# A hybrid attention block on one core: matmul operands moved to multiples of 256 bytes

## The chip, the cores and the metric

The kernel runs on one core of a Trainium2 chip. The metric is the device time of one execution in microseconds (us). A profile of one execution gives the times of single instructions. The engines are TensorE (PE in the rows, its weight loads PEld), VectorE (DVE), ScalarE (ACT), GpSimd (POOL) and SyncE (SP, which here only issues DMAs).

## The reference

One encoder layer over 512 tokens of width 1024 in float32, with 16 learned meta tokens placed ahead of them (528 rows in all):

```
h = rmsnorm(concat(meta, x));  proj = h @ w_in      # 1024 x 5120: q,k,v of two branches, two gates
A: neighbourhood attention, 8 heads of 64: each query sees 16 columns x 8 rows of the grid
   (8 x 64 tokens) with a learned bias, and the 16 meta tokens
B: differential attention, 4 heads: softmax(q1 k1) - lam * softmax(q2 k2) over all 528 keys,
   rotary positions, a norm per head
x = x + (sigmoid(g_na) * (A @ w_na) + sigmoid(g_df) * (B @ w_df)) @ w_o
x = x + (silu(h2 @ w_gate) * (h2 @ w_up)) @ w_down   # h2 = rmsnorm(x), inner width 2816
return rmsnorm(x) without the meta tokens
```

## The kernel before

Everything is held transposed: a tile has 128 features on the partitions and the tokens along the row. The host lays the tokens out column block by column block, 256 tokens, then the 16 meta tokens, then the other 256.

Every float32 factor of a dense product is split into a rounded high part and the remainder, both float32r, and one product is three matmuls (`mm3`, lines 137, 139, 141): high x high, high weight x low activation, low weight x high activation. Every matmul instruction loads its own 128x128 weights. Weights come in pieces of 8 blocks by DMA (`wraw`), and ACT and DVE split them (`whi`, `wlo`).

Names of the matmul groups, with the moving operand behind the arrow; all with 512 columns where nothing else is said:

- `pk<-xh` and `pv<-xh`: keys and values (`dense_full`), 528 tokens as two runs of 264 columns (`HALF`), 192 pairs each.
- `pq<-xh` (192) and `pg<-xh` (384): queries and gates (`dense_real`, `gate_block`). They need the 512 real tokens alone, so `rcols` reads two runs of 256 out of the row of 528, and results are handled as two runs (`v2`).
- `s<-kd`: scores. Branch B (line 506) takes two runs of 264 into two PSUM banks, 64 pairs; branch A (line 609) one run of 272, 64 matmuls.
- `tp`, `mp`: transposes of the softmax rows `w`. `pvd<-ath` (48) and `pvn<-ath` (64 of 256 columns): probabilities x values.
- `pd<-odh` (96), `pn<-onh` (96), `po<-mh` (192): output projections.
- `pf<-xgh`: gate and up of the feed-forward, 22 x 2 x 8 x 3 = 1056 matmuls. `pdn<-gh`: down, 462; `pdh<-gh`: its last block of outputs, 132 matmuls of 256 columns.

`xh` and `xl` are [128, 8, 528] float32r, so feature block k starts k x 2112 bytes into the tile.

The program has two phases. In the first (`run`), eight units (four heads of B, four pairs of heads of A, in turn) go through scores, softmax, transposes and value products in slots; between those PE does dense work of the next unit from a generator (`fill`). In the second (`phase_b`) the dense layers follow one another. The tile framework orders each engine's instructions, hands out addresses (pools stack up from the left end of a partition's row of SBUF or down from its right end) and makes a new tile in a tag wait until an old tile of that tag is free.

At the start `setup` loads x into eight tiles `xr` in the tags `ath` and `atl`, makes `xh`, `xl` and the sums of squares, and loads `lv` (the lambda vectors) into a tile of its own. `stats` makes the norm's factor `R` (from `ssq` by way of `ms`, `dg`, `rp`), folds it into the rotary tables `cos` and `sin`, finishes the first unit's keys and queries (`later`: rope by way of `sw`, then copies `kd` and `qs` by DMA), and multiplies the lambda vectors (`lt`, line 305). `build_bm` (POOL, line 593) adds bias (`toep`) and mask into `bm` for each head of branch A.

Of the kernel before, what the change touches and what calls it, by code (L numbers as in the profile page):

```python
# [18 lines left out]
P = 128  # L19
# [5 lines left out]
HALF = LT // 2  # L25
GRID_W = 64
# [9 lines left out]
KCOL = [0, 128, 272, 400]  # L36
MCOL = 256
# [13 lines left out]
V_PACK = [[(0, 64, 384), (64, 256, 0), (256, 264, 512)],  # L51
          [(0, 8, 520), (8, 200, 192), (200, 264, 448)]]
# [11 lines left out]
class Kernel:  # L64
# [133 lines left out]
    def setup(self):  # L198
        nc, a = self.nc, self.a
        cp, at = self.cp, self.attn  # L200
        self.unit_blocks = []
        for h in range(4):
            self.unit_blocks += [(16 + h, 12 + h, 20 + h), (4 + h, h, 8 + h)]
        self.wplan()

        vec = cp.tile([P, 25], F32, name="vec")
        nc.gpsimd.dma_start(vec, a["vec"])
        self.g1, self.g2, self.g3 = vec[:, 0:8], vec[:, 8:16], vec[:, 16:24]
        A1 = self.A1
# [23 lines left out]
        self.cos = at.tile([P, LT], F32, name="cos")  # L233
        self.sin = at.tile([P, LT], F32, name="sin")
# [10 lines left out]
        ssq = at.tile([P, LT], F32, name="ssq", tag="w", bufs=2)  # L245
        nc.scalar.activation(ssq, xr[0], AF.Square)
        for k in range(1, KT):
            sq = at.tile([P, LT], F32, name="sq", tag="e", bufs=3)
# [24 lines left out]
        self.R = A1.tile([P, LT], F32, name="R")  # L273
        self.na = 0
        self.nv = 0


    def stats(self, later):
# [8 lines left out]
        dg = self.attn.tile([P, LT], F32, name="dg", tag="e", bufs=3)  # L287
# [12 lines left out]
        lt = self.sm.tile([P, 2, 64], F32, name="lt")  # L300
# [12 lines left out]
    def dense_full(self, name, outs):  # L313
# [23 lines left out]
    def gate_block(self, dst, between=None):  # L337
# [7 lines left out]
        self.nc.vector.tensor_tensor(out=v2(dst), in0=v2(o[0]), in1=rcols(self.R), op=ALU.mult)  # L345
# [21 lines left out]
    def v_dense(self, st, diff):  # L367
# [11 lines left out]
    def v_transpose(self, st, diff):  # L379
# [3 lines left out]
        for c in range(NCH):  # L383
            k0 = KCOL[c] if diff else c * P
# [13 lines left out]
        k0 = MCOL if diff else T  # L398
        nc.tensor.transpose(mp[0:NMETA, :P], vt[:, k0:k0 + NMETA], self.ident)
# [26 lines left out]
    def k_dense(self, u, st, diff, defer=None):  # L426
# [24 lines left out]
    def q_dense(self, u, st, diff, defer=None):  # L451
# [40 lines left out]
    def d_scores(self, h, st, s):  # L492
# [11 lines left out]
        for i in range(2):  # L504
# [5 lines left out]
        e = at.tile([P, LT], F32, name="e", tag="e", bufs=3)  # L510
        nc.scalar.activation(e.rearrange("p (i n) -> p i n", i=2), sc[:, :, :HALF], AF.Exp, bias=m,  # L511
                             accum_out=l[:, c:c + 1])
        st["e"].append(e)
        if c == 1:
# [6 lines left out]
            w = at.tile([P, LT], F32, name="w", tag="w", bufs=2)  # L521
# [18 lines left out]
    def d_pv(self, h, st, am):  # L540
# [9 lines left out]
        sq = self.attn.tile([P, LT], F32, name="sqh", tag="e", bufs=3)  # L550
# [4 lines left out]
    def d_norm1(self, h, st, o, sq):  # L555
# [5 lines left out]
        dg = self.attn.tile([P, LT], F32, name="dg", tag="e", bufs=3)  # L561
# [11 lines left out]
    def build_bm(self, head):  # L573
# [4 lines left out]
        for b in range(4):  # L578
# [6 lines left out]
            nc.gpsimd.memset(bm[:, b, MCOL - lo:MCOL - lo + NMETA], 0.0)  # L585
# [12 lines left out]
    def n_scores(self, u, st, s):  # L598
# [11 lines left out]
        e = at.tile([P, LT], F32, name="en", tag="e", bufs=3)  # L610
# [7 lines left out]
        w = at.tile([P, LT], F32, name="w", tag="w", bufs=2)  # L618
# [23 lines left out]
    def n_pv(self, u, st, hd, am, ath, atl):  # L642
# [16 lines left out]
        tmp = self.attn.tile([P, LT], F32, name="otmp", tag="e", bufs=3)  # L659
# [72 lines left out]
    def run(self):  # L732
# [14 lines left out]
        self.attn = sat.enter_context(tc.tile_pool(name="attn", bufs=1))  # L747
        self.sstg = ExitStack()
# [49 lines left out]
    def phase_b(self, sA2):  # L798
        tc, nc, a = self.tc, self.nc, self.a
        with ExitStack() as top:  # L800
# [8 lines left out]
            for m in range(KT):  # L809
                nc.gpsimd.dma_start(v2(x1[:, m]), rcols(a["x"][m]))  # L810
# [170 lines left out]
def v2(t):  # L981
    return t.rearrange("p (b n) -> p b n", b=2)


def rcols(t):

    return bass.AP(t.tensor, t.offset, [list(t.ap[0]), [272, 2], [1, 256]])


# [14 lines left out]
def _layout(x, meta_tokens, mix_norm, w_in, na_rpb, lambda_q1, lambda_k1, lambda_q2, lambda_k2,  # L1004
# [4 lines left out]
    xc = np.concatenate([xp[:256], f(meta_tokens), xp[256:]], axis=0)  # L1009
# [6 lines left out]
    pos = np.concatenate([NMETA + perm[:256], np.arange(NMETA), NMETA + perm[256:]]).astype(np.float32)  # L1016
# [51 lines left out]
```

## Time and profile before

| | |
|---|---|
| median of 3 runs | 793.13 us (792.68 to 793.28) |
| the profiled execution | 792.06 us, its span 790.3 us |
| instructions in the span | 10578, of them 4002 matmuls |
| PE busy | 774.2 us (98%) |
| DVE, ACT, POOL busy | 460.2, 310.5, 65.4 us |
| mean DMA rate | 113 GB/s |

Matmuls are pipelined: a matmul of 512 columns takes some 390 ns from start to end in the trace, while the next one starts some 230 ns after it. The step from one start to the next is therefore what to read, not the duration.

### The profile page before, as it was taken

Reading aid. Unit: us, or ns where it says so; the run is one execution under the profiler, and the core shown is the slowest. Engines: PE = TensorE matmul, PEld = TensorE weight load, DVE = VectorE, ACT = ScalarE, POOL = GpSimd, SP = SyncE. Lnnn points to the kernel's source line nnn. Section 1 sums busy time; section 2 is a strip of 40 time slices with the busy share of each in tenths; the row PEclk is TensorE's granted clock in tenths of the full one; section 3 lists DMA queues with packets and bytes.
Section 4 is the critical chain, followed back from the end, with each engine's and each line's share of the span. In section 5 each row is a group of like instructions: output and inputs, shape, how many; then the busy total and the mean of one; then the engine's idle time right before and its main releaser. Section 6 shows DMA issues by size and latency. Waiting matters only on the chain.

```text
span 790.3 us, 10578 instructions
## 1 busy us (share of the span) xinstructions
PE 774.2 (98%) x4002; PEld 651.8 (82%) x4002; DVE 460.2 (58%) x892; ACT 310.5 (39%) x522; POOL 65.4 (8%) x140
## 2 busy tenths in 40 slices
PE   7999999999999999999999999999999999999995
PEld 5899889989898888878887888888888888888885
DVE  6868898798788766657443644444444545322314
ACT  6345554554555547323432432323232324322311
POOL 5300110110011000020220000000000000000100
PEclk9999999999999999999999999999999999999998
DMA  7474644434463412262232222332323234332313
GB/s 266 141 199 106 163 114 129 126 112 119 119 173 95 122 55 79 86 206 91 97 106 80 91 96 86 103 102 84 99 88 107 80 100 148 105 99 88 103 45 106
DMA packets 29922, 89.20 MB, mean 113 GB/s; under 512 B 4208, under 2 KB 6272, under 8 KB 29872
## 3 DMA queue, kind: packets, MB, share of 16 engines
q1 hardware_dynamic: 27904, 84.41, 35.3%
q0 software_dynamic: 1136, 3.34, 1.4%
q10 hardware_dynamic: 832, 0.79, 0.3%
q8 instruction: 31, 0.51, 0.3%
q14 instruction: 19, 0.16, 0.1%
HBM read 71.45 MB, written 2.10 MB: 93 GB/s over the span
## 4 chain that ended last, share of the span: by engine, by line
PE 95%; DVE 2%; DMA 1%; ACT 1%; issue 1%; SPq 0%; DVEq 0%; ACTq 0%
PE pf L137 10%; PE pf L141 10%; PE pf L139 10%; PE pdn L137 4%; PE pdn L139 4%; PE pdn L141 4%; PE pg L137 4%; PE pg L141 4%; PE pg L139 4%; PE s L506 2%; PE pq L141 2%; PE pv L137 2%; PE pv L139 2%; PE pv L141 2%; PE po L141 2%; PE po L137 2%
## 5 line engine op out<-in xcount | busy, mean ns | idle before, releaser
L114 ACT CAST whi<-wraw 128x1024 fp32r<-128x1024 f32 (+2 forms) x123 | 126.8, 1031 | 305.0 <-issue 112.7
L115 DVE TENSOR_TENSOR wlo<-wraw,whi 128x1024 fp32r<-128x1024 f32 (+2 forms) x123 | 147.5, 1199 | 89.4 <-ACT whi L114 84.7
L137 PE MATMUL pf<-xgh,whi 128*128 128x512 f32 x352 | 140.0, 398 | 0.0
L141 PE MATMUL pf<-xgh,wlo 128*128 128x512 f32 x352 | 139.2, 395 | 0.0
L139 PE MATMUL pf<-xgl,whi 128*128 128x512 f32 x352 | 139.2, 395 | 0.0
L139 PEld LDWEIGHTS pf<-xgl,whi 128*128 128x128 f32 x352 | 66.1, 188 | 16.1 <-issue 0.2
L141 PEld LDWEIGHTS pf<-xgh,wlo 128*128 128x128 f32 x352 | 66.1, 188 | 16.0
L137 PEld LDWEIGHTS pf<-xgh,whi 128*128 128x128 f32 x352 | 66.1, 188 | 15.9 <-issue 0.2
L139 PE MATMUL pdn<-gl,whi 128*128 128x512 f32 x154 | 59.9, 389 | 0.0
L137 PE MATMUL pdn<-gh,whi 128*128 128x512 f32 x154 | 59.9, 389 | 0.0
L141 PE MATMUL pdn<-gh,wlo 128*128 128x512 f32 x154 | 59.9, 389 | 0.0
L966 DVE TENSOR_TENSOR u<-pf,R 128x512 f32<-128x512 f32 x22 | 15.2, 691 | 68.8 <-PE pf L141 68.8
L137 PE MATMUL pg<-xh,whi 128*128 128x512 f32 x128 | 52.8, 412 | 0.4 <-DVE vt L374 0.4
L978 POOL TENSOR_TENSOR ssq<-ssq,sq 128x512 f32<-128x512 f32 x11 | 19.4, 1763 | 381.9 <-ACT sq L977 381.9
L139 PE MATMUL pg<-xl,whi 128*128 128x512 f32 x128 | 50.9, 397 | 0.0
L141 PE MATMUL pg<-xh,wlo 128*128 128x512 f32 x128 | 50.6, 395 | 0.0
L964 DVE TENSOR_TENSOR s<-pf,R 128x512 f32<-128x512 f32 x22 | 15.2, 690 | 45.1 <-PE pf L141 45.1
L147 ACT CAST ath<-tp 128x256 fp32r<-128x256 f32 (+1 forms) x48 | 20.5, 443 | 42.7 <-PE tp L631 22.0
L141 PEld LDWEIGHTS pdn<-gh,wlo 128*128 128x128 f32 x154 | 28.9, 188 | 6.1
L137 PEld LDWEIGHTS pdn<-gh,whi 128*128 128x128 f32 x154 | 28.9, 188 | 6.0
L139 PEld LDWEIGHTS pdn<-gl,whi 128*128 128x128 f32 x154 | 28.9, 188 | 5.9
L511 ACT ACTIVATE e<-s,m 128x528 f32<-128x528 f32 x32 | 22.5, 703 | 23.8 <-DVE m L509 23.4
(221 smaller groups left out, 1506.2 us busy)
## 6 DMA issues: line engine op xcount, KB each, us to landing
wraw<-in_w_in_dram SPq DMA_DIRECT2D x39, 512.0 KB, 3.5
wraw<-in_w_gate_dram SPq DMA_DIRECT2D x22, 512.0 KB, 3.2
wraw<-in_w_up_dram SPq DMA_DIRECT2D x22, 512.0 KB, 3.2
kd<-khl SPq DMA_DIRECT2D x32, 264.0 KB, 4.1
wraw<-in_w_down_dram SPq DMA_DIRECT2D x16, 512.0 KB, 3.5
qs<-qhl SPq DMA_DIRECT2D x32, 128.0 KB, 2.8
wraw<-in_w_o_dram SPq DMA_DIRECT2D x8, 512.0 KB, 3.3
wraw<-in_w_down_dram SPq DMA_DIRECT2D x8, 384.0 KB, 3.1
```

What stands on the lines that cost most here:

```text
L114: nc.scalar.copy(hi[:, k:k + h], raw[:, k:k + h])
L115: eng.tensor_tensor(out=lo[:, k:k + h], in0=raw[:, k:k + h], in1=hi[:, k:k + h].bitcast(F32), op=ALU.subtract)
L137: nc.tensor.matmul(outs[i], wh, rhs[i][0], start=start, stop=False)
L139: nc.tensor.matmul(outs[i], wh, rhs[i][1], start=False, stop=False)
L141: nc.tensor.matmul(outs[i], wl, rhs[i][0], start=False, stop=stop)
L147: self.nc.scalar.copy(hi, src)
L506: nc.tensor.matmul(sc[:, i, :HALF], qs[:, q], kd[:, p, i * HALF:(i + 1) * HALF], start=p == 0, stop=p == 1)
L511: nc.scalar.activation(e.rearrange("p (i n) -> p i n", i=2), sc[:, :, :HALF], AF.Exp, bias=m, accum_out=l[:, c:c + 1])
L964: nc.vector.tensor_tensor(out=s, in0=pgu[0], in1=R2, op=ALU.mult)
L966: nc.vector.tensor_tensor(out=u, in0=pgu[1], in1=R2, op=ALU.mult)
L978: (nc.gpsimd if m < n - 1 else nc.vector).tensor_tensor(out=ssq, in0=ssq, in1=sq, op=ALU.add)
```

## The change

Sizes and places in SBUF change; the arithmetic is the same but for the order of the keys. The meta tokens come last in the row, so the 512 real tokens are one run. Rows of 528 words that a matmul reads get a stride of 576 words (2304 bytes). Keys and values are computed in runs of 256 and 272 columns. The scores of branch B go into 528 neighbouring PSUM words that begin in the middle of one bank, so that run 0 ends that bank and run 1 begins the next, and DVE and ACT read them as one run. `cos`, `sin` and `R` share a tile in another pool; two of the eight `xr` tiles go to the tag `kd`; `lv` goes to the tag `toep` (one buffer) and `lt` to the tag `sw` (two buffers); a pad of 56 words is put at the right end of the row, under everything else there. Branch A keeps the meta keys in the middle of its key row (`NA_META`), with one more evacuation for it.

```diff
+LP = 576
+RUNS = [(0, 256), (256, 528)]
...
-        self.xh = A1.tile([P, KT, LT], F32R, name="xh")
-        self.xl = A1.tile([P, KT, LT], F32R, name="xl")
+        self.xh = A1.tile([P, KT, LP], F32R, name="xh")[:, :, :LT]
+        self.xl = A1.tile([P, KT, LP], F32R, name="xl")[:, :, :LT]
+        rows = A1.tile([P, 1600], F32, name="rows")[:, :3 * LT].rearrange("p (i n) -> p i n", i=3)
+        self.cos, self.sin, self.R = rows[:, 0], rows[:, 1], rows[:, 2]
...
-            xb = at.tile([P, 4, LT], F32, name="xr", tag=tag, bufs=1)
-            xr += [xb[:, i] for i in range(4)]
+            xb = at.tile([P, 3, LT], F32, name="xr", tag=tag, bufs=1)
+            xr += [xb[:, i] for i in range(3)]
+            xr.append(at.tile([P, LP], F32, name="xr", tag="kd", bufs=3)[:, :LT])
...
-        lv = self.sm.tile([P, 4, 64], F32, name="lv")
+        lv = at.tile([P, 4, 64], F32, name="lv", tag="toep", bufs=1)
...
-        lt = self.sm.tile([P, 2, 64], F32, name="lt")
+        lt = self.at_f32("lt", "sw", 2)[:, :P].rearrange("p (i n) -> p i n", i=2)
...
-        outs += [p[:, :HALF] for p in ps]
+        outs += [p[:, :b - a] for p, (a, b) in zip(ps, RUNS)]
         for k in range(KT):
             self.mm3(outs, wh[:, k], wl[:, k],
-                     [(self.xh[:, k, i * HALF:(i + 1) * HALF], self.xl[:, k, i * HALF:(i + 1) * HALF])
-                      for i in range(2)], k == 0, k == KT - 1)
+                     [(self.xh[:, k, a:b], self.xl[:, k, a:b]) for a, b in RUNS], k == 0, k == KT - 1)
...
-            self.mm3([o], wh[:, k], wl[:, k], [(rcols(self.xh[:, k]), rcols(self.xl[:, k]))],
+            self.mm3([ps], wh[:, k], wl[:, k], [(self.xh[:, k, :T], self.xl[:, k, :T])],
...
-            kd = self.attn.tile([P, 2, LT], F32R, name="kd", tag="kd", bufs=3)
+            kd = self.attn.tile([P, 2, LP], F32R, name="kd", tag="kd", bufs=3)[:, :, :LT]
...
-        for i in range(2):
+        sc = sc.rearrange("p i n -> p (i n)")[:, T - RUNS[0][1]:][:, :LT]
+        for r0, r1 in RUNS:
             for p in range(2):
-                nc.tensor.matmul(sc[:, i, :HALF], qs[:, q], kd[:, p, i * HALF:(i + 1) * HALF],
-                                 start=p == 0, stop=p == 1)
+                nc.tensor.matmul(sc[:, r0:r1], qs[:, q], kd[:, p, r0:r1], start=p == 0, stop=p == 1)
-        nc.vector.tensor_reduce(out=m, in_=sc[:, :, :HALF], op=ALU.max, axis=AX.XY, negate=True)
+        nc.vector.tensor_reduce(out=m, in_=sc, op=ALU.max, axis=AX.X, negate=True)
...
+        rp = es.enter_context(tc.tile_pool(name="rp", bufs=1, side="right"))
+        nc.gpsimd.memset(rp.tile([P, 56], F32, name="pad"), 0.0)
...
-                nc.gpsimd.dma_start(v2(x1[:, m]), rcols(a["x"][m]))
+                nc.gpsimd.dma_start(x1[:, m], a["x"][m][:, :T])
...
+    def at_f32(self, name, tag, bufs):
+        return self.attn.tile([P, LP], F32, name=name, tag=tag, bufs=bufs)[:, :LT]
```

The tiles in the tags `e`, `w` and `sw` are made by `at_f32` too. The value evacuation for branch A has 4 pieces in place of 6, the key evacuation 3 in place of 2.

## Rows read from the trace of the kernel before

**Rows 1.** The chain that ended last: shares of the span by engine.
```profile
PE 95%; DVE 2%; DMA 1%; ACT 1%; issue 1%; SPq 0%; DVEq 0%; ACTq 0%
```
**Rows 2.** What PE waited for, us in total, times, longest.
```profile
PE pq L141 <- DVE wlo L115: 1.4, 1, 1.4
```
**Rows 3.** Windows: busy us of PE, PEld, DVE, ACT, POOL; granted clock, DMA share, GB/s.
```profile
368.00:408.00 40.00, 40.00 (x179) 33.10 (x177) 19.70 (x23) 15.96 (x22) 10.73 (x6) 1.00 0.30 97
450.00:615.00 165.00, 165.00 (x708) 132.83 (x708) 74.46 (x89) 48.78 (x60) 0.00 (x0) 1.00 0.28 93
```
**Rows 4.** Timeline of PE, start and duration: `po` 64 matmuls, `pf` 62, first and last.
```profile
367.65 0.39 PE L141 MATMUL po<-mh,wlo 128*128 128x512 f32 x1
...
381.93 0.39 PE L141 MATMUL po<-mh,wlo 128*128 128x512 f32 x1
...
469.66 0.40 PE L141 MATMUL pf<-xgh,wlo 128*128 128x512 f32 x1
...
483.90 0.40 PE L137 MATMUL pf<-xgh,whi 128*128 128x512 f32 x1
```
**Rows 5.** Timeline of PE: 12 of `pvd`, 24 of `pg` (then `pvn`), 63 of `pd`.
```profile
84.41 0.39 PE L137 MATMUL pvd<-ath,vhl 128*128 128x512 f32 x1
...
86.98 0.39 PE L141 MATMUL pvd<-ath,vhl 128*128 128x512 f32 x1
...
308.65 0.39 PE L137 MATMUL pg<-xh,whi 128*128 128x512 f32 x1
...
314.21 0.39 PE L646 MATMUL pvn<-aM,VM 128*128 128x512 f32 x1
...
321.63 0.39 PE L137 MATMUL pd<-odh,whi 128*128 128x512 f32 x1
...
335.82 0.39 PE L141 MATMUL pd<-odh,wlo 128*128 128x512 f32 x1
```
**Rows 6.** Timeline of PE: 13 pairs of `pk`, 12 of `pv`, one of `s`, 25 `pdh`.
```profile
42.36 0.40 PE L141 MATMUL pk<-xh,wlo 128*128 128x264 f32 x2
...
45.29 0.41 PE L141 MATMUL pk<-xh,wlo 128*128 128x264 f32 x2
...
87.21 0.40 PE L137 MATMUL pv<-xh,whi 128*128 128x264 f32 x2
...
90.12 0.42 PE L609 MATMUL s<-kd,qs 128*128 128x272 f32 x2
90.37 0.38 PE L631 MATMUL tp<-ident,w 128*128 128x128 f32 x2
...
770.04 0.28 PE L141 MATMUL pdh<-gh,lo 128*128 128x256 f32 x1
...
772.84 0.28 PE L141 MATMUL pdh<-gh,lo 128*128 128x256 f32 x1
```
**Rows 7.** Timeline of the start, POOL and DVE.
```profile
11.59 5.50 POOL L593 TENSOR_TENSOR bm<-toep,mask 128x192 f32<-128x192 f32 x6 [4.67 <-DMA toep<-in_rpb_dram]
...
16.55 0.62 DVE L305 CUSTOM_DVE_ANT_0 lt<-lv 128x64 f32<-128x64 f32 x1
...
17.72 1.21 DVE L115 TENSOR_TENSOR wlo<-wraw,whi 128x1024 fp32r<-128x1024 f32 x1
...
19.48 0.21 DVE L305 CUSTOM_DVE_ANT_0 lt<-lv 128x64 f32<-128x64 f32 x1
...
19.77 5.69 POOL L593 TENSOR_TENSOR bm<-toep,mask 128x192 f32<-128x192 f32 x6 [1.82 <-DMA toep<-in_rpb_dram]
```
**Rows 8.** DMA issues: count, KB each, median us from issue to landing.
```profile
kd<-khl SPq DMA_DIRECT2D x32, 264.0 KB, 4.1
...
qs<-qhl SPq DMA_DIRECT2D x32, 128.0 KB, 2.8
```
**Rows 9.** Timeline of SP and PE at the first scores.
```profile
45.76 0.59 SPq L355 DMA_DIRECT2D qs<-qhl  x1
...
49.70 0.65 PE L506 MATMUL s<-kd,qs 128*128 128x264 f32 x4
```

More of the change, by code (lines that the diff above doesn't have):

```diff
@@ L34 @@
 LAM_INIT = 0.8 - 0.6 * math.exp(-0.3 * 0)
-KCOL = [0, 128, 272, 400]
-MCOL = 256
+KCOL = [0, 128, 256, 384]
+MCOL = T
+NA_META = 256
 NA_W = 272
@@ L49 @@
            [(80, 208, 0), (16, 80, 128), (208, 272, 192), (0, 16, 256)]]
-V_PACK = [[(0, 64, 384), (64, 256, 0), (256, 264, 512)],
-          [(0, 8, 520), (8, 200, 192), (200, 264, 448)]]
+V_PACK = [[(0, 64, 384), (64, 256, 0)], [(0, 192, 192), (192, 272, 448)]]
 GBLK = [(0, 1), (1, 2), (2, 3), (0, 3)]
@@ L232, in setup @@
         self.wemit = 2
-        self.cos = at.tile([P, LT], F32, name="cos")
-        self.sin = at.tile([P, LT], F32, name="sin")
         for k in range(KT):
@@ L243, in setup @@
         nc.sync.dma_start(self.sin, a["rope"][1])
-        ssq = at.tile([P, LT], F32, name="ssq", tag="w", bufs=2)
+        ssq = self.at_f32("ssq", "w", 2)
         nc.scalar.activation(ssq, xr[0], AF.Square)
         for k in range(1, KT):
-            sq = at.tile([P, LT], F32, name="sq", tag="e", bufs=3)
+            sq = self.at_f32("sq", "e", 3)
             nc.scalar.activation(sq, xr[k], AF.Square)
@@ L260, in setup @@
         make_identity(nc, self.ident)
-        lv = self.sm.tile([P, 4, 64], F32, name="lv")
+        lv = at.tile([P, 4, 64], F32, name="lv", tag="toep", bufs=1)
         nc.gpsimd.dma_start(lv, a["lam"].partition_broadcast(P))
-        self.mask = at.tile([P, 3, 4, 8], F32, name="mask")
+        self.mask = at.tile([P, 4, 4, 8], F32, name="mask")[:, 0:3]
         nc.gpsimd.dma_start(self.mask, a["mask"])
@@ L272, in setup @@
         self.lv = lv
-        self.R = A1.tile([P, LT], F32, name="R")
         self.na = 0
@@ L286, in stats @@
         yield 1.3
-        dg = self.attn.tile([P, LT], F32, name="dg", tag="e", bufs=3)
+        dg = self.at_f32("dg", "e", 3)
         self.diag(dg[:W].rearrange("p (c q) -> p c q", c=6), y, W, 6)
@@ L344, in gate_block @@
                 yield from between
-        self.nc.vector.tensor_tensor(out=v2(dst), in0=v2(o[0]), in1=rcols(self.R), op=ALU.mult)
+        self.nc.vector.tensor_tensor(out=dst, in0=o[0], in1=self.R[:, :T], op=ALU.mult)
         yield 0.65
@@ L371, in v_dense @@
         vt = self.stg.tile([P, LT], F32, name="vt", tag="vt", bufs=1)
-        for i in range(2):
-            for a, b, o in [(0, HALF, i * HALF)] if diff else V_PACK[i]:
+        for i, (lo, hi) in enumerate(RUNS):
+            for a, b, o in [(0, hi - lo, lo)] if diff else V_PACK[i]:
                 nc.vector.tensor_tensor(out=vt[:, o:o + b - a], in0=outs[i][:, a:b],
-                                        in1=self.R[:, i * HALF + a:i * HALF + b], op=ALU.mult)
+                                        in1=self.R[:, lo + a:lo + b], op=ALU.mult)
         st["vt"] = vt
@@ L383, in v_transpose @@
         for c in range(NCH):
-            k0 = KCOL[c] if diff else c * P
+            k0 = c * P
             nc.tensor.transpose(tp[:, c * P:(c + 1) * P], vt[:, k0:k0 + P], self.ident)
@@ L397, in v_transpose @@
         mp = self.tp.tile([P, T], F32, name="mpv", tag="tp")
-        k0 = MCOL if diff else T
-        nc.tensor.transpose(mp[0:NMETA, :P], vt[:, k0:k0 + NMETA], self.ident)
+        nc.tensor.transpose(mp[0:NMETA, :P], vt[:, T:T + NMETA], self.ident)
         if diff:
@@ L415, in rope @@
         nc = self.nc
-        sw = self.attn.tile([P, LT], F32, name="sw", tag="sw", bufs=2)
+        sw = self.at_f32("sw", "sw", 2)
         for i in range(4):
@@ L419, in rope @@
             nc.sync.dma_start(sw[32 * i:32 * i + 32, :n], raw[32 * j:32 * j + 32, :n])
-        shp = (lambda t: v2(t)) if n == T else (lambda t: t)
-        nc.vector.tensor_tensor(out=shp(raw[:, :n]), in0=shp(raw[:, :n]), in1=cos, op=ALU.mult)
-        nc.vector.tensor_tensor(out=shp(sw[:, :n]), in0=shp(sw[:, :n]), in1=sin, op=ALU.mult)
+        nc.vector.tensor_tensor(out=raw[:, :n], in0=raw[:, :n], in1=cos[:, :n], op=ALU.mult)
+        nc.vector.tensor_tensor(out=sw[:, :n], in0=sw[:, :n], in1=sin[:, :n], op=ALU.mult)
         nc.vector.tensor_tensor(out=raw[:, :n], in0=raw[:, :n], in1=sw[:, :n], op=ALU.add)
@@ L431, in k_dense @@
         raw = self.stg.tile([P, LT], F32, name="raw", tag="raw", bufs=2)
-        for i in range(2):
-            s = slice(i * HALF, (i + 1) * HALF)
+        for i, (a, b) in enumerate(RUNS):
             if diff:
-                nc.scalar.copy(raw[:, s], outs[i])
-            else:
-                nc.vector.tensor_tensor(out=raw[:, s], in0=outs[i], in1=self.R[:, s], op=ALU.mult)
+                nc.scalar.copy(raw[:, a:b], outs[i])
+                continue
+            for j, n, o in [(0, 256, 0)] if i == 0 else [(0, 256, NA_META + NMETA), (256, NMETA, NA_META)]:
+                nc.vector.tensor_tensor(out=raw[:, o:o + n], in0=outs[i][:, j:j + n],
+                                        in1=self.R[:, a + j:a + j + n], op=ALU.mult)
         def rest():
@@ L460, in q_dense @@
         else:
-            nc.vector.scalar_tensor_tensor(out=v2(raw), in0=v2(ps), scalar=0.125, in1=rcols(self.R),
+            nc.vector.scalar_tensor_tensor(out=raw, in0=ps, scalar=0.125, in1=self.R[:, :T],
                                            op0=ALU.mult, op1=ALU.mult)
@@ L465, in rest @@
             if diff:
-                self.rope(raw, qhl, rcols(self.cos), rcols(self.sin), T)
+                self.rope(raw, qhl, self.cos, self.sin, T)
             else:
@@ L503, in d_scores @@
         qs, kd = st["q"][c], st["k"][c]
-        for i in range(2):
+        sc = sc.rearrange("p i n -> p (i n)")[:, T - RUNS[0][1]:][:, :LT]
+        for r0, r1 in RUNS:
             for p in range(2):
-                nc.tensor.matmul(sc[:, i, :HALF], qs[:, q], kd[:, p, i * HALF:(i + 1) * HALF],
-                                 start=p == 0, stop=p == 1)
+                nc.tensor.matmul(sc[:, r0:r1], qs[:, q], kd[:, p, r0:r1], start=p == 0, stop=p == 1)
         m = self.sm.tile([P, 1], F32, name="m", tag="m", bufs=4)
-        nc.vector.tensor_reduce(out=m, in_=sc[:, :, :HALF], op=ALU.max, axis=AX.XY, negate=True)
-        e = at.tile([P, LT], F32, name="e", tag="e", bufs=3)
-        nc.scalar.activation(e.rearrange("p (i n) -> p i n", i=2), sc[:, :, :HALF], AF.Exp, bias=m,
+        nc.vector.tensor_reduce(out=m, in_=sc, op=ALU.max, axis=AX.X, negate=True)
+        e = self.at_f32("e", "e", 3)
+        nc.scalar.activation(e, sc, AF.Exp, bias=m,
                              accum_out=l[:, c:c + 1])
@@ L520, in d_scores @@
             nc.vector.tensor_tensor(out=st["l1"][:, b:b + 1], in0=l[:, 0:1], in1=l[:, 0:1], op=ALU.mult)
-            w = at.tile([P, LT], F32, name="w", tag="w", bufs=2)
+            w = self.at_f32("w", "w", 2)
             nc.vector.scalar_tensor_tensor(out=w, in0=e, scalar=r, in1=st["e"][0], op0=ALU.mult, op1=ALU.add)
@@ L549, in d_pv @@
         nc.scalar.copy(o, pv)
-        sq = self.attn.tile([P, LT], F32, name="sqh", tag="e", bufs=3)
+        sq = self.at_f32("sqh", "e", 3)
         nc.scalar.activation(sq[:, :T], o, AF.Square)
@@ L560, in d_norm1 @@
         y = self.rsqrt(ms[:, 0:4], SUB_EPS, st["l1"])
-        dg = self.attn.tile([P, LT], F32, name="dg", tag="e", bufs=3)
+        dg = self.at_f32("dg", "e", 3)
         self.diag(dg[:, :T].rearrange("p (c q) -> p c q", c=4), y, P, 4)
@@ L609, in n_scores @@
             nc.tensor.matmul(sc[:, :n], qs[:, b * P:(b + 1) * P], kd[:, p, lo:lo + n], start=p == 0, stop=p == 1)
-        e = at.tile([P, LT], F32, name="en", tag="e", bufs=3)
+        e = self.at_f32("en", "e", 3)
         m = self.sm.tile([P, 1], F32, name="m", tag="m", bufs=4)
@@ L617, in n_scores @@
         nc.vector.reciprocal(l[:, 1:2], l[:, 0:1])
-        w = at.tile([P, LT], F32, name="w", tag="w", bufs=2)
+        w = self.at_f32("w", "w", 2)
         for i, j, o in NA_PACK[b]:
@@ L658, in n_pv @@
         r = slice(64 * hd, 64 * hd + 64)
-        tmp = self.attn.tile([P, LT], F32, name="otmp", tag="e", bufs=3)
+        tmp = self.at_f32("otmp", "e", 3)
         nc.scalar.copy(tmp[r, :T], pv[64:128])
@@ L978, in sum_sq @@
             (nc.gpsimd if m < n - 1 else nc.vector).tensor_tensor(out=ssq, in0=ssq, in1=sq, op=ALU.add)
[L981 to L987, printed above, removed]
 _INS = ["x", "vec", "lam", "w_in", "rope", "mask", "rpb", "w_df", "w_na", "w_o", "w_gate", "w_up", "w_down"]
@@ L1008, in _layout @@
     xp = f(x)[0][perm]
-    xc = np.concatenate([xp[:256], f(meta_tokens), xp[256:]], axis=0)
+    xc = np.concatenate([xp, f(meta_tokens)], axis=0)
     xT = np.ascontiguousarray(xc.T.reshape(KT, P, LT))
@@ L1015, in _layout @@
     wi = _blocks(f(w_in)[0], 40)
-    pos = np.concatenate([NMETA + perm[:256], np.arange(NMETA), NMETA + perm[256:]]).astype(np.float32)
+    pos = np.concatenate([NMETA + perm, np.arange(NMETA)]).astype(np.float32)
     half = 32
```

3 lines of the change are left out of this document (1 added, 2 removed).

## The prediction

> **What bounds the kernel now.** I read the chain that ended last first: 95% of it is PE, and waits of other engines are a few per cent [rows 1]. The list of PE's waits is short; the one that the change can reach is the 1.4 us before `pq` at the start, for a weight split on DVE [rows 2]. The windows of the later stages show PE busy without a gap, at the full granted clock (1.00, the 2.4 GHz level), while DVE is busy about half of the time and ACT a third [rows 3]. So the time is, over most of the span, the number of matmuls times the step from one start to the next, and the question is what the change does to that step.
>
> The timeline gives the step. `po`: 64 matmuls from 367.65 to 381.93 us, 63 steps, 14.28 / 63 = 226.7 ns. `pf`, the same shape: 61 steps in 14.24 us, 233.4 ns [rows 4]. `pg`: 24 in 5.56 us, 231.7 ns; `pd`: 62 in 14.19 us, 228.9 ns; `pvd`: 11 in 2.57 us, 233.6 ns [rows 5]. Five groups of 512 columns, one clock, no waits, and steps that differ by up to 3%.
>
> What orders them is where the operands lie. Adding up tile sizes from the ends of SBUF's row: `mh` (read by `po`) starts at a multiple of 256 bytes and its blocks are 2048 bytes apart. `xgh` and `xgl` (read by `pf`) stack down from a right end that lies 224 bytes past such a multiple, and all that is stacked there in the second phase has sizes that are multiples, so all 1056 `pf` operands are 224 off. The blocks of `xh` and `xl` are 2112 bytes apart, 64 more than a multiple, so they are 0, 64, 128 or 192 off, and for `pg` and `pq` each is read in two runs. `ath` and `odh` lie 64 off, because `R` (2112 bytes) is under them; `vhl`, the weights of `pvd`, 128 off. Only the group that is at a multiple has the short step. The other explanation, that other engines hold PE back in the `pf` stage, has little for it: DVE is busy 19.70 of 40 us in a window of `po` and 74.46 of 165 in one of `pf`, ACT 15.96 and 48.78, DMA 0.30 and 0.28 [rows 3].
>
> **The change, part by part.** PE first.
>
> - `pf`. The 56-word pad is 224 bytes, so the right end becomes a multiple and `xgh`, `xgl` with it. 1056 x (233.4 - 226.7) = 7.1 us less [rows 4]. Lower bound: to the `pd` step only, 1056 x 4.5 = 4.8 [rows 4, 5].
> - `pg`, `pq`. One run of 512 at a multiple (stride 2304 bytes = 9 x 256): 576 x (231.7 - 226.7) = 2.9 us less; to the `pd` step only, 576 x 2.8 = 1.6 [rows 4, 5].
> - `pvd`, `pd`. `R` now sits in a tile of 6400 bytes, all tiles under and beside it are multiples: 48 x 6.9 + 96 x 2.2 = 0.5 us; at least nothing [rows 4, 5].
> - Pairs. `pk` takes 2.93 us for 12 pairs, 244 ns, `pv` 2.91 for 12, 242.5, a mean of 243.4. A run of 256 at a multiple takes 116.7 ns (`pdh`, 24 in 2.80 us), one of 272 125 (a pair of line 609 in 0.25 us): 241.7 together [rows 6]. 192 + 192 + 64 pairs x 1.7 = 0.8 us less. Both ends: nothing, as the rows have a resolution of 10 ns, or twice that, 1.6.
> - `pn`, `po`, `pdn` are at multiples already: nothing. `pdh` gets its weights to one, `pvn` its operands; no row shows that 256 columns would go below 116.7: nothing, or 196 x 2 ns = 0.4 at most.
>
> The other engines.
>
> - The start. `lt` takes a third tile of `sw` where two exist, so it waits for the first unit's rope, after 35 us; `lv` then holds the one buffer of `toep` until there, and with it the loads of bias and the first two `build_bm` on POOL, now at 11.59 and 19.77 us. Both leave the stretch in which DVE works towards the split that PE waits for. `lt` took 0.62 us there while POOL ran `bm`, and 0.21 us where it did not [rows 7]. Without it that split, at 17.72 us, can start some 0.6 us sooner, and more if POOL was holding other DVE work too; the wait is 1.4 us in all [rows 2]. I take 0.9 less, between 0 and 1.4. What follows (`ms`, `rsqrt`, `dg`, `rp`) starts from PE, so it moves along. The Trainium skill, page "SBUF — State Buffer", section "SBUF: two separate sides", says that VectorE and GpSimd take a shared pair of ports as an exclusive lock, for the whole instruction, when VectorE has two SBUF inputs; the 0.41 us between the two `lt` agrees. By it each of the seven two-input `xl` ahead of the split could have been held as well, which would use up the 1.4 us.
> - The late `lt`. Its two instructions now sit on DVE between rope of keys and rope of queries of the first unit; behind them wait the query's remainder, then the DMAs of `qs`, then the first scores. The last `qs` is issued at 45.76 us and lands some 2.8 later, 48.6, for scores at 49.70 [rows 8, 9]: 1.1 us of cover. I charge 0.3 of the 0.6 us, because PE also comes there sooner; 0 to 0.6.
> - The late `bm`. The first is needed by branch A's first scores, in the second unit, more than 20 us later than the two loads and 2 x 5.7 us of POOL work take after 38 us. It costs nothing while PE has dense work to fill with; what if it has not is the third rival.
> - The `kd` copies go into rows with a gap, two runs for one. They land after 4.1 us and are issued ahead of `qs` [rows 8, 9], so they have its cover and some more; a transfer longer by a quarter would use 1.0 of it. `x1` by one run for two, on POOL's queue, has the length of the output projection's start as cover. Nothing for both.
> - DVE: 4 units x (6 - 4) pieces of `vt` less, 4 x 1 of `raw` more, and single runs for double ones of the same length. DVE has half its time free [rows 3]. Nothing. The score tile as one run over two banks has the same 528 elements: nothing.
>
> Sum: -7.1 - 2.9 - 0.5 - 0.8 - 0.9 + 0.3 = -11.9 us. The profiled execution had 792.06 us (span 790.3, some 1.8 around it), so 780.2; the median of the runs is 1.07 above it, so 781.2 us.
>
> **The rivals.**
>
> 1. *The step does not hang on the address.* Then `pf` is slow for its stage's company, and only the start changes: 793.1 - 0.9 + 0.3 = 792.5 us. If what slows `pg` is that it reads two runs, its 2.9 us go as well: 789.6. Against it: `pd` and `pg`, a few microseconds apart, differ by 2.8 ns, and `po` is short with DVE as busy as in `pf` [rows 3, 5]. The Trainium skill stands on this side: "TensorE: Matmul & The Clock Gate", section "Back-to-back issue gap", gives a warm step as the columns over 2.4 GHz and 2.5 ns more, with no address in it; for 512 columns that is an estimate of 215.8 ns, under every row here, and by it all parts on PE save nothing. "SBUF — State Buffer", section "Specifications (TRN2)", has lines of 16 bytes, at which every operand starts already. The rows differ from both among groups of one length, so the measurement decides.
> 2. *The right side stays off.* If something else moves that end, `pf` keeps 233.4: 781.2 + 7.1 = 788.3 us. The sizes speak against it.
> 3. *Slower: the moved bias stalls the first unit's scores.* Twelve `bm` operations now fall where DVE makes remainders, maxima and weights of the first unit. If each holds one DVE instruction for the 0.41 us seen on `lt` [rows 7] and all of it reaches PE, that is 4.9 us, with the late `lt` 5.5: in place of the 0.3 charged that makes 781.2 + 5.2 = 786.4 us if the steps shrink, and 793.1 - 0.9 + 5.5 = 797.7 if they do not. It decides the sign only where PE's parts and the start give less than 5.5 us, that is, together with the first rival, or with more than half of all terms lost. For it: DVE is the busiest engine beside PE in the first phase. Against: PE has dense work between the slots, and its list of waits holds no entry of the first unit's scores.
>
> **How the numbers follow.** Forecast 0.86; first rival 0.08 (0.05 at 792.5, 0.03 at 789.6); the right side off 0.03; the third with no gain on PE 0.03. Range: the forecast's largest terms (7.4 for `pf`, as the last figure of a step is good to 0.2 ns, 3.1, 0.6, 1.6, 0.4, 1.4 and no charge) give -14.5, so 778.6; its smallest (4.8, 1.6, 0, 0, 0, and 0.6 charged) -5.8, so 787.3, above the bias stall with full gain. I give 778 to 787.5, which leaves out the 0.14 of the three rivals. A difference under 0.2% (1.6 us) can't be told from none here. Faster by more: 0.86 + 0.03 + 0.03 = 0.92; within: 0.05; slower: 0.03.
>
> **What would show it.** In the profile after: `pf`, `pg`, `pq`, `pvd` and `pd` at steps of 226 to 227 ns in the timeline, like `po`; the stretch of `pf` 7 us shorter, the first phase with the start nearly 5 (2.9 + 0.5 + 0.8 + 0.6); PE's wait for `wlo` before `pq` shorter than 1.4 us; `lt` after 35 us and `bm` after it; no new wait of PE for `s`, `tp` or `mp`. The prediction is wrong if `pf` keeps a step above 230 with its tiles at multiples, or if the list of PE's waits has new entries of several us in the first unit.

## The result and the profile after

The changed kernel takes 784.22 us (median of 4 runs, 782.45 to 785.38) beside 793.2 us for the kernel before on the same chip (4 runs, 792.68 to 793.74). The ratio is 0.9885, 95% interval 0.9863 to 0.9906: 1.15% or 9.0 us faster. The forecast of 781.2 us was 3 us too low; its range of 778 to 787.5 us holds the result. The profiled execution took 784.85 us (span 783.1), 7.2 us less than that of before (792.06).

The page of the changed kernel, busy time and the chain that ended last:
```profile
PE 768.4 (98%) x4002; PEld 654.0 (84%) x4002; DVE 457.5 (58%) x888; ACT 310.4 (40%) x522; POOL 58.3 (7%) x141
...
PE 92%; DVE 4%; DMA 2%; SPq 1%; issue 1%; ACT 0%; DVEq 0%; ACTq 0%
```
PE is still what the time consists of, as in [rows 1]. Its list of waits (us in total, times, longest):
```profile
PE pk L142 <- ACT xh L246: 2.7, 1, 2.7
PE rp L944 <- DVE dg L189: 1.7, 1, 1.7
...
PE pg L142 <- DVE vt L381: 0.4, 1, 0.4
```
The wait for `wlo` of [rows 2] is gone, and no entry for `s`, `tp` or `mp` has come. So whatever changed after the start changed in the step from one matmul to the next. The timeline of PE in the changed kernel, first and last rows of stretches without a gap (start, duration):
```profile
315.07 0.40 PE L144 MATMUL pg<-xl,whi 128*128 128x512 f32 x1
...
316.23 0.39 PE L142 MATMUL pg<-xh,whi 128*128 128x512 f32 x1
...
320.08 0.39 PE L146 MATMUL pg<-xh,wlo 128*128 128x512 f32 x1
320.31 0.39 PE L142 MATMUL pd<-odh,whi 128*128 128x512 f32 x1
...
336.85 0.39 PE L144 MATMUL pd<-odl,whi 128*128 128x512 f32 x1
...
469.72 0.39 PE L144 MATMUL pf<-xgl,whi 128*128 128x512 f32 x1
...
483.77 0.39 PE L142 MATMUL pf<-xgh,whi 128*128 128x512 f32 x1
```
`pf`: 62 steps in 14.05 us, 226.6 ns, where [rows 4] had 233.4. `pd`: 73 steps in 16.54 us, 226.6 ns, for the 228.9 of [rows 5]. `pg` shows what the forecast did not have. These rows follow a run of `pvn` of 256 columns and begin with the second `pg` behind it: the first 5 steps take 1.16 us, 232 ns each, the next 17 take 3.85 us, 226.5 ns.

Steps and their sums per group, from the starts of all its matmuls in the two profiled executions:

| group | step before, ns | step after, ns | sum of all steps, us | forecast, us |
|---|---|---|---|---|
| `pf` x1056 | 233.3 | 226.7 | 247.13 to 240.21: -6.92 | -7.1 |
| `pg` x384, `pq` x192 | 231.6 | 229.9 | 135.58 to 134.72: -0.86 | -2.9 |
| `pvd` x48, `pd` x96 | 233.2, 229.0 | 228.4, 226.7 | 35.48 to 35.02: -0.46 | -0.5 |
| `pdh` x132, `pvn` x64 (256 columns) | 116.8, 116.2 | 119.8, 118.6 | 27.51 to 27.97: +0.46 | 0 |
| pairs of `pk`, of `pv`; `s` in the sum | 243.9, 243.5 | 244.2, 244.1 | 116.17 to 116.42: +0.25 | -0.8 |
| `po`, `pdn` | 226.7 | 226.7 | none | 0 |

(The start is left out of `pq` and `pk`.) Where each kernel stands at the same matmul gives the same account: the two are level after the start (19.33 and 19.34 us), and the changed kernel leads by 0.9 us when `pf` begins, by 7.8 when `pf` has ended and by 7.5 at the last `pdh`; 0.3 of that is lost behind it, which leaves the 7.2 between the two spans.

The start. The timeline of DVE in the kernel before:
```profile
9.93 5.66 DVE L237 SCALAR_TENSOR_TENSOR xl<-xr,vec,xh 128x528 fp32r<-128x528 f32 x7
15.52 1.11 DVE L250 TENSOR_TENSOR ssq<-ssq,sq 128x528 f32<-128x528 f32 x1
```
and the timelines of ACT, PE and DVE in the changed one:
```profile
9.00 0.62 ACT L119 CAST whi<-wraw 128x512 fp32r<-128x512 f32 x1 [3.31 <-DMA wraw<-in_w_in_dram]
...
10.31 0.81 PE L142 MATMUL pk<-xh,whi 128*128 128x256 f32 x2 [2.75 <-ACT xh L246]
...
10.29 2.80 DVE L247 SCALAR_TENSOR_TENSOR xl<-xr,vec,xh 128x528 fp32r<-128x528 f32 x4
...
15.37 1.52 DVE L260 TENSOR_TENSOR ssq<-ssq,sq 128x528 f32<-128x528 f32 x2
16.80 1.22 DVE L120 TENSOR_TENSOR wlo<-wraw,whi 128x1024 fp32r<-128x1024 f32 x1
...
18.63 0.40 PE L142 MATMUL pq<-xh,whi 128*128 128x512 f32 x1
...
19.34 0.40 PE L142 MATMUL pq<-xh,whi 128*128 128x512 f32 x1
```
The split that PE waited for starts at 16.80 us, 0.9 sooner than in [rows 7], as counted on. An `xl` takes 0.70 us (2.80 / 4); the seven of the kernel before, the later of which ran beside `bm` (from 11.59 us [rows 7]), took 0.81 on average (5.66 / 7). An `ssq` takes 0.76 us where one beside `bm` took 1.11, and `lt` is gone. But PE itself came later. The windows of 2 us say why (PE, PEld, DVE, ACT, POOL busy; granted clock, DMA share, GB/s), first the kernel before:
```profile
10.00:12.00 2.00, 1.97 (x7) 1.67 (x8) 2.00 (x4) 1.95 (x4) 0.41 (x1) 0.50 1.04 407
12.00:14.00 2.00, 2.00 (x13) 2.00 (x13) 1.95 (x3) 2.00 (x4) 2.00 (x3) 0.64 1.03 410
14.00:16.00 2.00, 2.00 (x19) 2.00 (x18) 2.00 (x4) 2.00 (x4) 2.00 (x3) 1.00 1.03 417
```
and then the changed one:
```profile
12.00:14.00 2.00, 2.00 (x11) 2.00 (x11) 1.76 (x3) 2.00 (x5) 0.00 (x0) 0.50 1.04 415
14.00:16.00 2.00, 2.00 (x11) 2.00 (x11) 2.00 (x4) 2.00 (x4) 0.00 (x0) 0.50 1.00 403
16.00:18.00 2.00, 2.00 (x15) 2.00 (x15) 1.90 (x4) 2.00 (x4) 0.00 (x0) 0.79 0.36 147
```
POOL's `bm` is gone from here, but the granted clock, which reads 0.50 once PE goes on after its wait for `xh`, stays there (the 1.2 GHz level) until 16.8 us instead of 13.4, as the 0.79 and the 0.64 of the last window that it reaches into give. PE starts 11 matmuls in a window where it had started 13 and 19. Both kernels start their next `pq` after the split at the same time, 19.33 and 19.34 us.

The late `lt` and `bm` cost nothing that can be seen. The changed kernel's DVE and POOL:
```profile
38.15 0.22 DVE L314 CUSTOM_DVE_ANT_0 lt<-lv 128x64 f32<-128x64 f32 x1
...
43.83 2.84 POOL L601 TENSOR_TENSOR bm<-toep,mask 128x192 f32<-128x192 f32 x6 [3.19 <-DMA toep<-in_rpb_dram]
```
`lt` takes 0.22 us where its first took 0.62, six `bm` 2.84 us instead of 5.50 [rows 7].

### The profile page after: what moved, and what is told of

Same layout as the page of the kernel before. It is cut to its first block, busy times and chain, and to the rows that moved or that the text cites. A ratio compares the mean times of both kernels' runs of the same rounds, so it can differ in the third digit from the quotient of the medians.

```text
span 783.1 us, 10564 instructions
## 1 busy us (share of the span) xinstructions
PE 768.4 (98%) x4002; PEld 654.0 (84%) x4002; DVE 457.5 (58%) x888; ACT 310.4 (40%) x522; POOL 58.3 (7%) x141
## 4 chain that ended last, share of the span: by engine, by line
PE 92%; DVE 4%; DMA 2%; SPq 1%; issue 1%; ACT 0%; DVEq 0%; ACTq 0%
PE pf L142 10%; PE pf L144 10%; PE pf L146 10%; PE pdn L146 4%; PE pdn L142 4%; PE pdn L144 4%; PE pg L142 4%; PE pg L144 4%; PE pg L146 4%; PE s L515 2%; PE po L146 2%; PE po L144 2%; PE po L142 2%; PE pq L142 2%; PE pq L144 2%; PE pq L146 2%
## 5 line engine op out<-in xcount | busy, mean ns | idle before, releaser
L142 PE MATMUL pf<-xgh,whi 128*128 128x512 f32 x352 | 137.7, 391 | 0.0
L144 PE MATMUL pf<-xgl,whi 128*128 128x512 f32 x352 | 137.0, 389 | 0.0
L146 PE MATMUL pf<-xgh,wlo 128*128 128x512 f32 x352 | 137.0, 389 | 0.0
L142 PE MATMUL pk<-xh,whi 128*128 128x256 f32 (+1 forms) x128 | 29.2, 306 | 2.7 <-ACT xh L246 2.7
```

What stands on the lines that cost most here:

```text
L142: nc.tensor.matmul(outs[i], wh, rhs[i][0], start=start, stop=False)
L144: nc.tensor.matmul(outs[i], wh, rhs[i][1], start=False, stop=False)
L146: nc.tensor.matmul(outs[i], wl, rhs[i][0], start=False, stop=stop)
```

## The experiments

Unless said otherwise the edits are to the changed kernel, and the kernel before was timed beside each (medians 793.14 to 793.44).

**The pad alone, on the kernel before.**
```diff
+        rp = es.enter_context(tc.tile_pool(name="rp", bufs=1, side="right"))
+        nc.gpsimd.memset(rp.tile([P, 56], F32, name="pad"), 0.0)
```


> The kernel before with one line more, the 56-word pad at the right end. If the step of a matmul hangs on where its operands lie, the 1056 pf steps go from 233.4 to 226.7 ns and take 7 us off; the 132 pdh of 256 columns, whose weights the pad also moves to multiples of 256 bytes, go from 116.7 to 119.8 ns as in the profile after and give 0.4 back: 6.5 us less than before, some 786.6. pg, pq, pvd, pd and the start stay as before. If pf was slow for the company of its stage: no change, 793.

Measured: 786.16 us (4 runs), ratio 0.9915 (0.9902 to 0.9929), 7.0 us faster. `pf` has 226.7 ns a step, 240.21 us in sum, as in the changed kernel; `pg`, `pd` and `pvd` keep 231.8, 229.0 and 233.5. Two lines that put 224 bytes at the end of a row, and no other work, carry over three quarters of the gain. The first rival, that the step does not hang on the address, falls.

**The change without the pad.**
```diff
-        rp = es.enter_context(tc.tile_pool(name="rp", bufs=1, side="right"))
-        nc.gpsimd.memset(rp.tile([P, 56], F32, name="pad"), 0.0)
```


> The changed kernel without the pad, everything on the left still at multiples of 256 bytes. By the address theory pf goes back to 233.4 ns and pdh to 116.7: 6.5 us more than the changed kernel, 790 to 791, so all that the left side and the start are worth is 2 to 3 us of the 9. If the left side carries the gain, it stays near 784.

Measured: 790.58 us (9 runs), ratio 0.9973 (0.9963 to 0.9983), 2.6 us faster. `pf` is back at 233.3 (247.13 us), `pdh` at 116.8; `pg` and `pd` keep 229.9 and 226.7. The two halves add up: 7.0 + 2.6 = 9.6 beside 9.0 together. In this kernel's profiled execution the start went another way, and its timeline shows how:
```profile
6.19 0.62 ACT L119 CAST whi<-wraw 128x512 fp32r<-128x512 f32 x1 [0.47 <-DMA wraw<-in_w_in_dram]
...
15.51 0.50 PE L142 MATMUL pq<-xh,whi 128*128 128x512 f32 x1 [0.24 <-ACT whi L119]
15.71 1.22 DVE L120 TENSOR_TENSOR wlo<-wraw,whi 128x1024 fp32r<-128x1024 f32 x1
17.32 0.40 PE L142 MATMUL pq<-xh,whi 128*128 128x512 f32 x1
```
The second half of the first weight piece was there at 6.19 us instead of 9.00, PE waited 0.5 us for `xh` instead of 2.7, the granted clock is 1.00 in every window from 8 to 20 us, and the next `pq` starts at 17.32 us, 2.0 sooner than in either profile above. Taking out the pad changes nothing at the start. In the profiled executions of the changed kernel, of this one and of the four runs below that change only the pad or `pf`, this `pq` starts between 17.32 and 19.34 us: the start varies by 2 us from one execution to another.

**Other pads: `xgh`, `xgl` at 32, 64 and 128 bytes past a multiple.** One run each.
```diff
-        nc.gpsimd.memset(rp.tile([P, 56], F32, name="pad"), 0.0)
+        nc.gpsimd.memset(rp.tile([P, 48], F32, name="pad"), 0.0)   # 40 and 24 in the other two
```


> The changed kernel with a pad of 48 words, so that all on the right lies 32 bytes past a multiple of 256. Address theory: pf above 226.7 ns, between 228 and 234. If only an offset of 224 was bad: 226.7. The weights of pdh lie 32 off as well: if it is their place that made pdh 119.8 in place of 116.7, it is near 116.7 again.

> The same with a pad of 40 words, 64 bytes past a multiple. pd had 228.9 ns at this offset in the kernel before with weights at multiples: pf 229, 2.4 us more than the changed kernel. Rival: 226.7 or 233.4, if offset was not what set pd.

> The same with a pad of 24 words, 128 bytes past a multiple. Address theory: pf above 226.7 ns, between 228 and 234; by the rival, that only a stage's company counts, 226.7.

The timeline of PE, first and last `pf` of one stretch. At 32 bytes, 61 matmuls:
```profile
469.82 0.40 PE L142 MATMUL pf<-xgh,whi 128*128 128x512 f32 x1
...
483.82 0.40 PE L142 MATMUL pf<-xgh,whi 128*128 128x512 f32 x1
```
At 64 bytes, 63:
```profile
469.71 0.39 PE L146 MATMUL pf<-xgh,wlo 128*128 128x512 f32 x1
...
483.90 0.39 PE L144 MATMUL pf<-xgl,whi 128*128 128x512 f32 x1
```
At 128 bytes, 62:
```profile
469.63 0.39 PE L146 MATMUL pf<-xgh,wlo 128*128 128x512 f32 x1
...
483.79 0.40 PE L142 MATMUL pf<-xgh,whi 128*128 128x512 f32 x1
```
That is 14.00 / 60 = 233.3 ns, 14.19 / 62 = 228.9 and 14.16 / 61 = 232.1 (232.4 over all 1056). With the two kernels of the case:

| bytes past a multiple of 256 | 0 | 32 | 64 | 128 | 224 |
|---|---|---|---|---|---|
| `pf` step, ns | 226.7 | 233.3 | 228.9 | 232.4 | 233.3 |
| the profiled execution, us | 784.85 | 791.27 | 785.3 | 790.03 | (no pad) 789.56 |
| `pdh` step, ns (its weights lie there) | 119.8 | 118.3 | 114.7 | 118.9 | 116.8 |

Five addresses, the same instructions, at three places in the table over 232 ns. (The executions also differ by their starts.) The pad moves the tiles that the other engines use on that side as well, `x1` among them; that these set the step is unlikely, as `po` and `pdn`, beside which those tiles are written, keep 226.7 ns at all five. 64 bytes off is the `pd` of before, whose 228.9 had been taken as the bound of the forecast: it is the step of that address. The order is not that of the distance (128 is worse than 64), and no run here says why. `pdh` reads its moving operand at a multiple in all of them; its weights are not best there.

**A change of shape put into `pf`.** In 80 places of the steady `pf` stretch one matmul of 512 columns is issued as two of 256.
```diff
+                        if f > 1 and k in (2, 6):
+                            nc.tensor.matmul(ps, wh[:, k], xgh[:, k], start=False, stop=False)
+                            for i in range(2):
+                                t = slice(256 * i, 256 * i + 256)
+                                nc.tensor.matmul(ps[:, t], wh[:, k], xgl[:, k, t], start=False, stop=False)
+                            nc.tensor.matmul(ps, wl[:, k], xgh[:, k], start=False, stop=False)
+                            continue
```


> The changed kernel, with 2 of each 24 pf matmuls of 512 columns done as two of 256 columns on the same operands (80 places, same sums). Theory of the settling: after matmuls of another shape the steps of a run need several matmuls to come back to 226.7 ns, as after the scores in the first phase (233, 236, 229, 232, 231, 227), and that is why pg and pq kept 229.9 there with operands at multiples. Then each place costs about 12 ns for the two halves and some 25 to 30 ns after them: 3.1 us more than the changed kernel, and the pf steps behind a place are above 230. Rival: pg and pq are held by the other engines and DMAs of the first phase. Then pf goes back to 226.7 at once, and the 80 places cost 1 us.

Measured: 786.83 us (6 runs), ratio 0.9921 (0.9908 to 0.9934); the sum of `pf` is 242.84 us, 2.63 more than without, 33 ns a place. The timeline of PE after one place:
```profile
471.81 0.40 PE L874 MATMUL pf<-xgl,whi 128*128 128x256 f32 x2
472.04 0.40 PE L875 MATMUL pf<-xgh,wlo 128*128 128x512 f32 x1
...
473.20 0.39 PE L144 MATMUL pf<-xgl,whi 128*128 128x512 f32 x1
...
474.33 0.39 PE L871 MATMUL pf<-xgh,whi 128*128 128x512 f32 x1
```
The two halves take 0.23 us together, the 5 steps after them 1.16 us (232 ns each), the next 5 1.13 (226). All operands are at multiples. So it is the change of shape that lengthens the steps behind it, as in the rows of `pg` above.

**More warm-up ahead of the first matmul**, to keep the clock from falling at the start.
```diff
-WARM = 3
+WARM = 9
```


> The changed kernel with 9 warm-up matmuls on zeros in place of 3, which fill the stretch from 7.5 to 10 us in which PE has nothing; no work is left out. In the profile after the granted clock was at its half level from 10.0 to 16.9 us, in that of before from 10.0 to 13.4. If PE's clock in that stretch is what the start costs, the first 24 pairs of pk end near 15.5 us instead of 18.6, and the time falls by 1 to 2 us; the runs also scatter less than 782.5 to 785.4. If PE then waits for the weight split, which ends at 18.0 us in the profile after, the gain is 0.6 us at most.

Measured: 783.95 us (783.79 to 784.26), ratio 0.9886 (0.9872 to 0.9899). The granted clock is 1.00 in every window from 8 to 20 us, and the spread of the runs falls from 2.9 to 0.5 us, but the median is only 0.3 us below the changed kernel's: the smaller of the two outcomes that were expected. PE's waits and the timeline:
```profile
PE pq L146 <- DVE wlo L120: 0.7, 1, 0.7
...
16.87 0.39 PE L142 MATMUL pq<-xh,whi 128*128 128x512 f32 x1
16.95 1.22 DVE L120 TENSOR_TENSOR wlo<-wraw,whi 128x1024 fp32r<-128x1024 f32 x1
```
PE now comes at 16.87 us and meets the wait for the split again: DVE is the next limit.

**The moved `lv` and `lt` alone, on the kernel before.**
```diff
-        lv = self.sm.tile([P, 4, 64], F32, name="lv")
+        lv = at.tile([P, 4, 64], F32, name="lv", tag="toep", bufs=1)
-        lt = self.sm.tile([P, 2, 64], F32, name="lt")
+        lt = self.attn.tile([P, LT], F32, name="lt", tag="sw", bufs=2)[:, :P].rearrange("p (i n) -> p i n", i=2)
```


> The kernel before with the lambda vectors in the tag toep and their products in the tag sw, and nothing else: all offsets modulo 256 stay. It isolates the start. If the moved lt and bm work is what lets the first weight split on DVE end sooner, that split starts near 16.8 us in place of 17.7, PE's wait for it before pq falls from 1.4 us to under 0.8, and the time falls by 0.5 to 1.5 us. Rival: the start is set by when the second half of the first weight piece lands (between 6 and 9 us in the runs so far) and by PE's clock behind that; then the time stays within 0.5 us of before, or moves only with that landing.

Measured: 792.64 us (11 runs, 790.96 to 793.2) beside 793.25 (15 runs), ratio 0.9991 (0.9982 to 1.0): 0.6 us, under the 0.2% that can be told from nothing, so the time does not decide. The split starts at 17.00 us, 0.7 sooner, and the wait for it is gone, but that of `pk` for `xh` is 3.2 us in the profiled execution, and the granted clock falls behind it (0.59 and 0.56 in the windows 12 to 14 and 14 to 16 us).

**The second weight half split later**, so that its late landing does not hold up `xh`.
```diff
+            if k == 2:
+                self.split(hi0[:, 4:], lo0[:, 4:], raw0[:, 4:])
```


> The changed kernel with the split of the second half of the first weight piece put behind the third of the eight x blocks on ACT and DVE instead of ahead of the second. If ACT's wait in order for that landing is what leaves PE without work until 9.5 to 10.3 us, PE gets its second block near 7 us, the granted clock does not fall for so long, and the time falls by 1 to 2 us from 784.2, with less scatter. If x itself lands late, nothing changes.

Measured: 783.88 us (782.01 to 784.2), ratio 0.9877 (0.9864 to 0.9891). The 782.01 us are the profiled execution, with the clock at 1.00 throughout and the next `pq` at 17.35 us; the other three are within 0.4 us of the changed kernel's median. No clear gain. The edit did not put the idea to the test: in this profile the half was there at 6.49 us, and ACT takes two blocks of x ahead of it, not three. In the profile of the next run, with the same edit, the half lands late (9.11 us) and ACT waits 2.8 us for it with six blocks to go.

**Late half, `WARM` of 6, and the weights of `pdh` 64 bytes off** (a tile of 48 words behind the last weights), the late half as above.
```diff
-WARM = 3
+WARM = 6
+            nc.gpsimd.memset(W2.tile([P, 48], F32, name="pad2"), 0.0)
```

> The changed kernel with that late half, 6 warm-up matmuls in place of 3, and the last layer's weight tiles (W2) 64 bytes past a multiple of 256, where pdh took 114.7 ns in place of 119.8. 132 x 5.1 ns = 0.7 us for pdh, and what the late half brings: 782 us; the warm-up adds something only if PE still has a hole there.

Measured: 783.01 us (782.43 to 783.28), ratio 0.987 (0.9857 to 0.9883). It has the lowest median of all, 1.2 us under the changed kernel, but the intervals overlap. `pdh` went to 117.0 ns, not to the 114.7 of the run at 64 bytes: the place of the weights alone does not fix this step. In the run at 64 bytes it even changes on the way, with the weights 64 bytes off throughout:
```profile
767.80 0.28 PE L146 MATMUL pdh<-gh,lo 128*128 128x256 f32 x1
...
769.39 0.28 PE L144 MATMUL pdh<-gl,hi 128*128 128x256 f32 x1
769.74 0.47 PE L146 MATMUL pdh<-gh,lo 128*128 128x256 f32 x1
770.05 0.28 PE L142 MATMUL pdh<-gh,hi 128*128 128x256 f32 x1
...
772.40 0.28 PE L146 MATMUL pdh<-gh,lo 128*128 128x256 f32 x1
```
14 steps in 1.59 us (113.6 ns), an interruption by two `rp`, then 20 in 2.35 (117.5). The present run has the same two steps: 117.8 ns until the `ms` in the middle of the second half of `pdh`, then
```profile
765.20 0.28 PE L144 MATMUL pdh<-gl,hi 128*128 128x256 f32 x1
...
767.58 0.28 PE L144 MATMUL pdh<-gl,hi 128*128 128x256 f32 x1
```
21 steps in 2.38 us (113.3), and 117.8 again behind its two `rp`. With the weights 64 off there are two steps, and both runs change from one to the other only where matmuls of another shape come between; the two means differ by how long each step lasted. Why is open.

## Why the prediction held, point by point

- **`pf`, "1056 x (233.4 - 226.7) = 7.1 us less": right.** 6.92 by its steps, 7.0 by the pad alone. Shown by the pad, by its removal and by three other pads. The page "TensorE: Matmul & The Clock Gate" of the Trainium skill, section "Back-to-back issue gap", by which an isolated step is the columns over the clock and a constant, with no address in it, does not agree: at one clock and 512 columns these rows have 226.7 to 233.3 ns, by the address alone.
- **`pg`, `pq`, "One run of 512 at a multiple ... 2.9 us less": the step that failed, by size.** It measured 0.86. The address does what was said (226.5 ns once settled), but in the first phase dense work is cut by scores, `pvn` and transposes, and the first steps after each cut are long. Between 36 and 355 us both traces have some 80 stretches of `pg` or `pq` that begin after another shape, half of them 4 steps long or shorter. Mean steps by place in the stretch, from the starts of all their matmuls (behind the first place, steps over 400 ns are left out):

| place in the stretch | steps | before, ns | after, ns |
|---|---|---|---|
| first | 80 | 282.7 | 281.9 |
| 2 to 4 | 188 | 231.8 | 232.1 |
| 5 to 9 | 164 | 231.8 | 229.3 |
| from the tenth on | 110 | 231.7 | 226.9 |

Only the last row gains the 5 ns of the forecast. Places 2 to 4 gain nothing and 5 to 9 half; the first step, some 50 ns longer than the others, gains 0.8 ns. At 5 ns a step the first four places make 1.3 us of the 2.0 missing and the next five 0.4. That it is the change of shape that makes the steps behind a cut long is shown in `pf`; here the cuts themselves were not taken out. The rate was taken from `po`, which runs uncut; `pg`'s own stage, with its cuts, should have been counted.
- **`pvd`, `pd`: right**, 0.46 of 0.5, though `pvd`, in stretches of twelve, stays at 228.4 ns.
- **Pairs, "a mean of 243.4 ... 241.7 together": wrong.** The 116.7 ns for a run of 256 came from `pdh`, whose weights then lay 224 bytes off. The changed kernel's `pk`, where it has its runs one at a time, shows what the two cost at multiples:
```profile
39.39 0.28 PE L144 MATMUL pk<-xl,whi 128*128 128x256 f32 x1
...
40.35 0.28 PE L142 MATMUL pk<-xh,whi 128*128 128x256 f32 x1
...
40.93 0.28 PE L144 MATMUL pk<-xl,whi 128*128 128x272 f32 x1
...
41.93 0.29 PE L142 MATMUL pk<-xh,whi 128*128 128x272 f32 x1
```
8 steps in 0.96 us, 120 ns, and 8 in 1.00, 125: 245 together, no less than the 243.4 of two runs of 264. `pk`, `pv` and `s` got 0.25 us longer in sum.
- **`pdh`, `pvn`, "nothing, or 196 x 2 ns = 0.4 at most": wrong in sign**, 0.46 us more. Steps of 256 columns got longer with every operand at a multiple, and the bound had allowed for a gain alone.
- **The start, "I take 0.9 less, between 0 and 1.4": within its bounds, mis-sized.** The split starts 0.9 us sooner, by the mechanism given. In the profiled execution it is worth nothing, as PE came later with half a clock; with the two tiles alone the median gained 0.6, which can't be told from nothing. The forecast took PE's arrival as fixed; it hangs on when the weight half lands (ACT starts on it between 6.19 and 9.56 us in these profiles) and on the clock after the pause. That more warm-up keeps the clock at 1.00 and shrinks the spread is shown. What makes the half land early or late was not tried.
- **The late `lt`, "I charge 0.3": nothing to be seen.** The third rival falls with it: no wait of the first unit's scores is in the list.

Added up, the misses are 0.2 for `pf`, 2.0, 1.1 for the pairs, 0.5, 0.9 for the start and -0.3 for `lt`, 4.4 us. The profiled execution was 784.85 where 780.2 were forecast, 4.65 more; the rest is the 0.3 behind the last `pdh`. What was looked for as "the first phase with the start nearly 5" came out at 0.9. The medians differ by 1.8 us more than the profiled executions do (9.0 and 7.2), of the size by which the start varies; that the median came within 3 us of the forecast is in part luck.

## What to carry to other kernels

When matmuls of one shape run at different steps in stages where nothing waits, add up the tiles and look at the operands' addresses: one pad of 224 bytes gained 7 of the 9 us here. Take the step for an estimate from a stage that is cut by other shapes as often as yours, and never from another width or another placing of the weights. A wait that is removed at the start is only worth what the next arrival allows: look at the clock and the landing of the DMAs there, and at more than one execution.

## What the runs showed that was not expected

- After a change of shape, some five steps of 512 columns take 232 ns instead of 226.7, 33 ns a place in the `pf` experiment; after the transposes the first step is longer still (94.55 to 94.86 us, 310 ns):
```profile
94.55 0.48 PE L142 MATMUL pg<-xh,whi 128*128 128x512 f32 x1
94.86 0.40 PE L144 MATMUL pg<-xl,whi 128*128 128x512 f32 x1
```
- Of the five places tried, 512 columns are fastest at a multiple of 256 bytes (226.7 ns), next best 64 off (228.9), and 32, 128 and 224 off are all above 232. 256 columns with everything at a multiple are the slowest of their kind (119.8 ns, against 114.7 to 118.9 with the weights off it), and with the weights 64 off they have two steps, 113.3 and 117.8 ns. Why is open; a version of the first phase with its weights off a multiple was not tried.
